# One-block buffers for streamed weight rows, and a second table stage whose activation loads and products are queued behind the first

## The chip, the cores and the metric

The kernel runs on one core of one Trainium2 chip. The metric is device time in microseconds (us) of one execution, as the median of several runs of the same program; lower is better. The engines are named as the profile names them: PE is the matrix engine and PEld its weight load, DVE the vector engine, ACT the scalar engine, POOL the engine that issues the gathers here, SP the engine that issues most of the other transfers. SPq and ACTq are the instruction queues of SP and ACT, which issue DMAs in order.

## The reference, cut to what matters

Two layers. Each layer runs four mixers on 512 tokens (256 context, 256 latent), then a feed-forward network that chooses experts by product keys. Only the feed-forward part and the weight loads are touched.

```python
def block(xb):                                   # 128 tokens at a time
    qry = (xb @ wq).reshape(PEER_BLOCK, PEER_HEADS, 2, PEER_DKEY)
    s = jnp.einsum('thpk,hpnk->thpn', qry, sub_keys)
    sv, si = lax.top_k(s, PEER_TOPK)
    ...
    eidx = jnp.take_along_axis(cand_i, fpos, axis=-1)   # 16384 experts, 8 heads x 16 chosen
    gate = jax.nn.softmax(fs, axis=-1)
    act = jax.nn.gelu(jnp.einsum('td,thkd->thk', xb, u[eidx]), approximate=False)
    w = gate * act
    return jnp.einsum('thk,thkd->td', w, v[eidx])
```

The modulation of each layer, silu(c) @ w_ada + b_ada, is a second product of which the kernel does some columns inside the feed-forward stage of layer 0. The last layer's feed-forward part runs on the 256 latent tokens alone.

## The kernel before

The feed-forward part is computed densely: all 16384 experts, as 128 blocks of 128, for most tokens. It has two table stages. In the **first table's stage** (`u_blocks`) the rows of u are multiplied with the tokens: for each block of 128 experts, 24 matmuls (8 pieces of the model width, each in three products of high and low halves), then a gelu on ACT; two blocks make a pair, and the pair's activations go to a DRAM scratch `ad` by a DMA that ACT issues. In the **second table's stage** (`v_blocks`) a pair's activations come back from `ad` into the tile `va`, the gates come from another DRAM scratch `gd` into `vg`, DVE multiplies them, ACT and DVE split the product into a high and a low half (`wt`), and PE multiplies with the rows of v into eight accumulators `f`.

Rows of both tables come from HBM into the tile `raw`. ACT copies them to a rounded high half and DVE subtracts to get the low half (tiles `spl`, 10 buffers of one block each, shared in the first stage with gathered rows). `raw` has two buffers of 1 MB, each for two blocks in the table stages and for one 256-column weight chunk elsewhere (`wdma`).

The first tokens of each layer (128 in layer 0, 32 in layer 1, `APART`) are not in the dense product. Their chosen rows are gathered one per partition by POOL (`tokens_apart`), 256 gathers in layer 0: DVE makes a dot product with a u row (line 1415) or adds a scaled v row to `facc` (line 1422). `rows_to` decides how many gathers have been written into the program by each pair: 144 of layer 0's (`PHASE1`) by the end of the first table's stage, the rest over the second.

While the first stage runs, DVE and PE also build the gates (`gate_hot`, `gates`), which go to `gd`. In layer 0 the second stage carries 32 rows of the modulation (`ada_row`): a 512 KB load `adaw` and one or two DVE products each, with the constant `csb` (1 MB) loaded and passed through a sigmoid ahead of them.

The order within each engine's queue is made by a planner, which simulates the program and may move an instruction ahead of those written before it. `pin` puts an instruction behind the one written just before it on its engine. Instructions on an engine run in order, so one that waits holds back all behind it. Before the change the loads and products of `v_blocks` and the load of `csb` aren't pinned.

Of the kernel before, what the change touches and what calls it, by code (L numbers as in the profile page):

```python
# [18 lines left out]
L = 2  # L19
# [5 lines left out]
MAGIC = 12582912.0  # L25
GSCALE = 32768.0

RAW, SPL, WQS = 2, 10, (6, 5)
AHEAD = 3
PIECE = 3  # L30
F_ML, F_NA, F_MLA, F_SW = (1.3, 2.0), (1.0, 1.2), (1.2, 1.2), (1.2, 1.0)
# [22 lines left out]
class Kernel:  # L54
# [39 lines left out]
    def build(self):  # L94
        tc, nc, A = self.tc, self.nc, self.A
        with ExitStack() as es:
            self.cst = es.enter_context(tc.tile_pool(name="cst", bufs=1))
            self.dram = es.enter_context(tc.tile_pool(name="scr", bufs=1, space=bass.MemoryType.DRAM))
            self.raw = es.enter_context(tc.tile_pool(name="raw", bufs=RAW, reuse_waits="tile"))
            self.spl = es.enter_context(tc.tile_pool(name="spl", bufs=SPL, reuse_waits="tile"))  # L100
            cst = self.cst
            self.xt = cst.tile([128, KD, TA], F32, name="xt")
            self.cc = cst.tile([128, KD, 2], F32, name="cc")
            nc.sync.dma_start(self.cc, A["cc"])
            self.con = cst.tile([128, C_N], F32, name="con")
            nc.sync.dma_start(self.con[:, 0:128], A["con"][:, 0:128])
            self.ident = self.con[:, C_ID:C_ID + 128]
            self.ng = cst.tile([128, 5, KD], F32, name="ng")
            nc.scalar.dma_start(self.ng, A["ng"])
            self.badat = cst.tile([128, L, 6, KD], F32, name="badat")  # L110
            nc.scalar.dma_start(self.badat, A["bada"])
            self.small = cst.tile([128, 64], F32, name="small")
            nc.scalar.dma_start(self.small, A["small"])
            self.ones = cst.tile([128, 128], F32, name="ones")
            nc.vector.memset(self.ones, 1.0)
            self.mhalf = cst.tile([128, 4], F32, name="mhalf")
            nc.gpsimd.memset(self.mhalf, -0.5)
            self.cmb = cst.tile([4, 2], F32, name="cmb")
            nc.vector.tensor_add(self.cmb, self.ident[0:4, 0:2], self.ident[0:4, 2:4])
            self.mod = {}  # L120
            self.ms = cst.tile([128, 4], F32, name="ms")
            self.wd = [TA - APART[0], TC - APART[1]]
            self.gd = [self.dram.tile([self.wd[l] // 32, 128, 128, 32], F32, name=f"gd{l}") for l in range(L)]
            self.ad = [self.dram.tile([128, 128, self.wd[l]], F32, name=f"ad{l}") for l in range(L)]
            for l in range(L):
                self.mixers(l)
                if self.stop == ("mix", l):
                    return
                self.peer(l)
                if self.stop == ("peer", l):  # L130
                    return
            self.final()
# [162 lines left out]
    def ada_row(self, w, junk, csb, l, n, nv):  # L295

        nc = self.nc
        if l not in self.mod:
            self.mod[l] = self.cst.tile([128, 6, KD, 2], F32, name=f"mod{l}")
            nc.gpsimd.memset(self.mod[l], 0.0)  # L300
        s, k = divmod(n, KD)
        nc.sync.dma_start(w, self.A["wadat"][l, n])
        for j in range(nv):
            o = self.mod[l][:, s, k, j:j + 1]
            self.pin(nc.vector.scalar_tensor_tensor(junk, w, 1.0, csb[:, j], op0=ALU.mult, op1=ALU.mult, accum_out=o))
        nc.vector.tensor_add(self.mod[l][:, s, k, :nv], self.mod[l][:, s, k, :nv], self.badat[:, l, s, k:k + 1].to_broadcast([128, nv]))
# [83 lines left out]


    def raw_tile(self):
        return self.wraw.tile([128, 2048], F32, name="raw")

    def spl_tile(self):
        return self.wspl.tile([128, 1024], F32R, name="spl")

    def wdma(self, src, nk=KD):
        w = self.raw_tile().rearrange("p (k c) -> p k c", c=256)
        self.nc.sync.dma_start(w[:, :nk], src)  # L400
        return w

    def pin(self, ins, on=True):
        return self.tc.keep_in_program_order(ins) if on else ins

    def gload(self, src):

        w = self.raw_tile()[:, 0:1024].rearrange("p (k c) -> p k c", c=128)
        self.nc.sync.dma_start(w, src[:, :, 0:128])
        return w  # L410

# [631 lines left out]
    def peer(self, l):  # L1043
# [7 lines left out]
        with ExitStack() as es:  # L1051
# [19 lines left out]
            with ExitStack() as e1:  # L1071
# [4 lines left out]
                with ExitStack() as e2:  # L1076
                    ep2 = e2.enter_context
                    self.s = ep2(tc.tile_pool(name=f"ps_s{l}", bufs=QS[l], reuse_waits="tile"))
                    self.sm = ep2(tc.tile_pool(name=f"ps_sm{l}", bufs=2, reuse_waits="tile"))
                    local = [ep2(tc.tile_pool(name=f"ps_{n}{l}", bufs=b, reuse_waits="tile")) for n, b in (("wr", 2), ("ws", WQS[l]))]  # L1080
                    kp = ep2(tc.tile_pool(name=f"ps_k{l}", bufs=1, reuse_waits="tile"))
                    self.psum = ep2(tc.tile_pool(name=f"ps_p{l}", bufs=3, space=PSUM, reuse_waits="tile"))
                    psk = ep2(tc.tile_pool(name=f"ps_psk{l}", bufs=3, space=PSUM, reuse_waits="tile"))
# [33 lines left out]
                with ExitStack() as e2:  # L1117
# [24 lines left out]

                    def u_next():
                        u_pair()
                        rows_to(PHASE1[l] * (used[0] - u0) // (64 - u0))
                    for n, _ in enumerate(routes[t0]):
                        if n % RN[l] == 0:
                            u_next()
# [30 lines left out]
                with ExitStack() as e2:  # L1179
# [3 lines left out]
                    acc = [pf.tile([128, 512], F32, name=f"f{d}") for d in range(KD)]  # L1183
                    extra = []
                    if l == 0:
                        self.csb = self.vp.tile([128, 2, 1024], F32, name="csb", bufs=1)
                        nc.sync.dma_start(self.csb, A["ccb"])
                        for j in range(2):
                            sgb = self.junk
                            self.pin(nc.scalar.activation(sgb, self.csb[:, j], AF.Sigmoid))  # L1190
                            nc.vector.tensor_mul(self.csb[:, j], self.csb[:, j], sgb)
                        extra = [(0, n, 2) for n in range(40, 48)] + [(1, n, 2) for n in range(16)] + [(1, n, 1) for n in range(40, 48)]
                    if apart:
                        rows = ep2(tc.tile_pool(name=f"rows{l}", bufs=ROWS, reuse_waits="tile"))
# [1 line left out]
                    for n, i in enumerate(self.v_order(l)):  # L1196
                        rows_to(PHASE1[l] + (2 * apart - PHASE1[l]) * n // 58 if n < 58 else 300)
                        self.v_blocks(l, n, i, acc, ts, w - wd)
                        if extra and n % 2 == 0:
                            self.ada_row(self.vp.tile([128, 1024], F32, name="adaw", bufs=1), self.junk, self.csb, *extra.pop(0))  # L1200
            for k in range(KD):
                self.dump(f"xp{l}_{k}", self.xt[:, k])
# [234 lines left out]
    def u_prep(self, l):  # L1437
# [3 lines left out]
        if n == 128:  # L1441
            return
        self.unext += 1
        if n % 2 == 0:
            self.u = self.raw.tile([128, 2048], F32, name="raw").rearrange("p (b k e) -> p b k e", b=2, k=KD)
            nc.sync.dma_start(self.u, self.A["ut"][l, n:n + 2].rearrange("b p k e -> p b k e"))
        uh, ul = (self.spl.tile([128, 1024], F32R, name="spl").rearrange("p (k e) -> p k e", k=KD) for _ in range(2))
        self.pin(nc.scalar.copy(uh, self.u[:, n % 2]), n < 3)  # L1448
        self.pin(nc.vector.tensor_tensor(ul, self.u[:, n % 2], uh.bitcast(F32), op=ALU.subtract), n < 3)  # L1449
        self.uparts.append((uh, ul))  # L1450

    def u_blocks(self, l, i, hh, hl, w):
# [12 lines left out]
                self.mm3(ps[:, :w], uh[:, k], ul[:, k], hh[k], hl[k], k == 0, k == KD - 1)  # L1465
            nc.scalar.activation(a[:, b, :w], ps[:, :w], AF.Gelu)  # L1466
        if not fold:
            nc.scalar.dma_start(self.ad[l][i:i + 2].rearrange("b p t -> p b t"), a[:, :, :w])

    def v_order(self, l):  # L1470

# [9 lines left out]
    def v_blocks(self, l, n, i, acc, ts, off):  # L1481
# [3 lines left out]
        q = slice(off, off + w)  # L1485
        parts = []
        nc, vp = self.nc, self.vp
        v = self.raw.tile([128, 2048], F32, name="raw").rearrange("p (b d) -> p b d", b=2)
        nc.sync.dma_start(v, self.A["v"][l, i:i + 2].rearrange("b p d -> p b d"))
        fold = i < 2 * FOLD[l]  # L1490
        a = self.kept[:, i:i + 2] if fold else vp.tile([128, 2, w], F32, name="va")
        if i % 4 == 0 and not fold:
            self.vg = vp.tile([128, w // 32, 4, 32], F32, name="vg", bufs=2)
            nc.sync.dma_start(self.vg[:, :w // 32].rearrange("p q b t -> p q (b t)"),
                              self.gd[l][:, :, i:i + 4].rearrange("q p b t -> p q (b t)"))
        if not fold:
            nc.sync.dma_start(a[:, :, :w], self.ad[l][i:i + 2].rearrange("b p t -> p b t"))
        wide = l > 0
        wt = vp.tile([128, 2, 2, w], F32R, name="wt")
        wh, wl = wt[:, :, 0], wt[:, :, 1]  # L1500
        if not fold:
            av = a[:, :, :w].rearrange("p b (q t) -> p b q t", t=32)
            nc.vector.tensor_mul(av, av, self.vg[:, :w // 32, i % 4:i % 4 + 2].rearrange("p q b t -> p b q t"))  # L1503
        nc.scalar.copy(wh, a[:, :, :w])
        nc.vector.tensor_tensor(wl, a[:, :, :w], wh.bitcast(F32), op=ALU.subtract)  # L1505
        for b in range(2):
            vh, vl = (self.spl.tile([128, 1024], F32R, name="spl") for _ in range(2))
            nc.scalar.copy(vh, v[:, b])  # L1508
            nc.vector.tensor_tensor(vl, v[:, b], vh.bitcast(F32), op=ALU.subtract)  # L1509
            parts.append((vh, vl, wh[:, b], wl[:, b], wt[:, b].rearrange("p a t -> p (a t)")))  # L1510

        def mm(d, b):
# [73 lines left out]
class Halves:  # L1586
# [5 lines left out]
    def __getitem__(self, x):  # L1592
        if isinstance(x, slice):
            t = self.tiles[x.start // 4]
            return t[:, x.start % 4:x.start % 4 + x.stop - x.start]
        return self.tiles[x[1] // 4][(x[0], x[1] % 4) + tuple(x[2:])]


# [219 lines left out]
```

## Time and profile before

| | us |
|---|---|
| median of 3 runs | 2793.98 |
| lowest and highest run | 2786.86, 2801.69 |
| profiled execution: its own time | 2801.05 |
| profiled execution: span from first to last instruction | 2799.3 |
| PE busy in it | 2628.3 |
| mean granted PE clock (share of full speed) | 0.973 |

The profiled execution is 1.75 us longer than its span and 7.07 us above the median of the runs. In the order of time the span holds: layer 0 mixers to about 450 us, its query and first table's stage to 1175, its second table's stage to about 1700, layer 1 mixers to about 2000, its first stage to about 2429 and its second to about 2780. An idle PE in a stage is time that another engine or a transfer set; the busy share alone doesn't tell which.

### The profile page before, as it was taken

What the parts mean: (1) busy time and instruction counts of PE and PEld (TensorE: products, weight loads), DVE (VectorE), ACT (ScalarE), POOL (GpSimd) and SP (SyncE); (2) the same over time, 40 slices, a digit from 0 to 9 for tenths busy, and PEclk for the clock granted to TensorE, in tenths of its full rate; (3) what the DMA queues carried; (4) which work ended last, traced back from release to release, by engine and by line L of the source; (5) the groups of instructions that cost most, each with busy time, mean ns of one, the idle gap of its engine ahead of it and who ended that gap; (6) DMA issues with size and microseconds to landing.
All of it is one profiled execution on the core that took longest, in us unless ns stands there. A gap on an engine that the chain in (4) does not pass through costs nothing. (4 is left out here: it accounts for less than half of the span.)

```text
span 2799.3 us, 44568 instructions
## 1 busy us (share of the span) xinstructions
PE 2628.3 (94%) x17143; PEld 2407.9 (86%) x17143; DVE 2168.7 (77%) x4499; ACT 1249.8 (45%) x2059; POOL 490.9 (18%) x419
## 2 busy tenths in 40 slices
PE   8989899999999999799999998988999999998998
PEld 5766768999998898799999997767899999898987
DVE  5665757999998886699999886565788777677776
ACT  4564645334344433343333334554545444444443
POOL 0010000003443234233333320000001111111110
PEclk9999899999999999899999999999999999999999
DMA  7110424647998989989999993211535787998984
GB/s 264 69 61 31 166 89 157 220 159 246 347 359 337 340 321 378 338 322 386 382 367 384 372 364 125 76 39 68 201 137 191 270 283 282 333 319 294 333 306 167
DMA packets 275733, 691.48 MB, mean 247 GB/s; under 512 B 18016, under 2 KB 145376, under 8 KB 266048
## 3 DMA queue, kind: packets, MB, share of 16 engines
q1 hardware_dynamic: 196608, 448.12, 45.6%
q0 software_dynamic: 46080, 167.79, 15.9%
q10 hardware_dynamic: 32832, 72.72, 6.9%
q8 instruction: 134, 2.20, 0.3%
q14 instruction: 79, 0.65, 0.1%
HBM read 616.56 MB, written 71.57 MB: 246 GB/s over the span
## 5 line engine op out<-in xcount | busy, mean ns | idle before, releaser
L72 PE MATMUL pu<-h2h,spl 128*128 128x384 f32 (+1 forms) x2048 | 637.8, 311 | 37.1 <-ACT spl L1448 28.0
L74 PE MATMUL pu<-h2h,spl 128*128 128x384 f32 (+1 forms) x2048 | 629.6, 308 | 2.9 <-DVE spl L1449 2.9
L73 PE MATMUL pu<-h2l,spl 128*128 128x384 f32 (+1 forms) x2048 | 630.2, 308 | 0.0
L72 PEld LDWEIGHTS pu<-h2h,spl 128*128 128x128 f32 x2048 | 394.2, 192 | 44.9 <-ACT spl L1448 32.7
L74 PEld LDWEIGHTS pu<-h2h,spl 128*128 128x128 f32 x2048 | 393.5, 192 | 4.8 <-DVE spl L1449 4.6
L73 PEld LDWEIGHTS pu<-h2l,spl 128*128 128x128 f32 x2048 | 394.2, 192 | 0.3
L1509 DVE TENSOR_TENSOR spl<-raw,spl 128x1024 fp32r<-128x1024 f32 x256 | 305.7, 1220 | 98.2 <-ACT spl L1508 92.5
L1448 ACT CAST spl<-raw 128x1024 fp32r<-128x1024 f32 x256 | 266.3, 1051 | 249.2 <-DMA raw<-in_ut 92.3
L1508 ACT CAST spl<-raw 128x1024 fp32r<-128x1024 f32 x256 | 261.9, 1051 | 256.5 <-DMA raw<-in_v 173.6
L1449 DVE TENSOR_TENSOR spl<-raw,spl 128x1024 fp32r<-128x1024 f32 x256 | 311.7, 1224 | 44.1 <-ACT spl L1448 32.6
L73 PE MATMUL f<-wt,spl 128*128 128x384 f32 x1024 | 343.2, 335 | 0.0
L74 PE MATMUL f<-wt,spl 128*128 128x384 f32 x1024 | 336.3, 334 | 0.0
L72 PE MATMUL f<-wt,spl 128*128 128x384 f32 x1024 | 288.4, 337 | 2.1 <-ACT spl L1508 1.9
L1519 PE MATMUL f<-wt,spl 128*128 128x448 f32 x1024 | 251.1, 372 | 17.1 <-ACT spl L1508 11.7
L1409 POOL DMA_INDIRECT spl<-in_un,ix x97 | 131.6, 1357 | 704.8 <-DVE fp L1263 241.6
L1466 ACT ACTIVATE act<-pu 128x384 f32<-128x384 f32 (+1 forms) x216 | 93.7, 436 | 299.3 <-PE pu L74 268.8
L1519 PEld LDWEIGHTS f<-wt,spl 128*128 128x128 f32 x1024 | 186.0, 190 | 33.3 <-ACT spl L1508 15.0
L427 DVE TENSOR_TENSOR spl<-raw,spl 128x512 fp32r<-128x512 f32 (+1 forms) x226 | 149.8, 702 | 64.0 <-ACT spl L423 55.0
L73 PEld LDWEIGHTS f<-wt,spl 128*128 128x128 f32 x1024 | 193.0, 188 | 0.5 <-issue 0.5
L74 PEld LDWEIGHTS f<-wt,spl 128*128 128x128 f32 x1024 | 191.6, 188 | 0.0
L72 PEld LDWEIGHTS f<-wt,spl 128*128 128x128 f32 x1024 | 187.9, 189 | 3.2 <-ACT spl L1508 2.2
L1409 POOL DMA_INDIRECT row<-in_vn,ix x87 | 125.7, 1445 | 369.6 <-DVE facc L1422 313.0
(326 smaller groups left out, 5029.2 us busy)
## 6 DMA issues: line engine op xcount, KB each, us to landing
raw<-in_ut SPq DMA_DIRECT2D x128, 1024.0 KB
raw<-in_v SPq DMA_DIRECT2D x128, 1024.0 KB
ad<-act ACTq DMA_DIRECT2D x64, 384.0 KB
gd<-gstage ACTq DMA_DIRECT2D x12, 2048.0 KB
vg<-gd SPq DMA_DIRECT2D x32, 768.0 KB
va<-ad SPq DMA_DIRECT2D x64, 384.0 KB
raw<-in_win SPq DMA_DIRECT2D x22, 1024.0 KB
raw<-in_wq SPq DMA_DIRECT2D x16, 1024.0 KB
```

Of the source, the lines that this page charges most:

```text
L72: mm(ps, ah, bh, start=first, stop=False, **kw)
L73: mm(ps, ah, bl, start=False, stop=False, **kw)
L74: mm(ps, al, bh, start=False, stop=last, **kw)
L427: return eng.tensor_tensor(p[1][o], w[:, o], p[0][o].bitcast(F32), op=ALU.subtract)
L1409: nc.gpsimd.indirect_dma_start(r, None, tabs[which], bass.IndirectOffsetOnAxis(ix[:, s:s + 1], 0))
L1448: self.pin(nc.scalar.copy(uh, self.u[:, n % 2]), n < 3)
L1449: self.pin(nc.vector.tensor_tensor(ul, self.u[:, n % 2], uh.bitcast(F32), op=ALU.subtract), n < 3)
L1466: nc.scalar.activation(a[:, b, :w], ps[:, :w], AF.Gelu)
L1508: nc.scalar.copy(vh, v[:, b])
L1509: nc.vector.tensor_tensor(vl, v[:, b], vh.bitcast(F32), op=ALU.subtract)
L1519: nc.tensor.matmul(acc[d][:, off:off + 2 * w], vh[:, c], both, start=first, stop=last)
```

## The change

- `raw` becomes four buffers of 512 KB, one block each, in the same memory. Each block of u and of v has a load of its own; weight chunks are loaded as two halves (`wdma` returns `Halves`).
- The scratch `ad` is laid out so that the two blocks of a pair lie side by side in each partition: a run of 3072 bytes in layer 0 and 1792 in layer 1, where there were two runs of half that.
- In the second table's stage the loads of `vg` and `va`, the product on DVE and the split of the product on ACT and DVE are pinned for the first two pairs; the loads and splits of the rows of v are not.
- The load of `csb` and its sigmoid move from ahead of the second stage to behind its second pair, pinned; the modulation rows start at the third pair, with one at pair 3 besides the even ones (32 as before), and their loads are pinned.
- `rows_to` in the first stage reaches its 144 gathers (26 in layer 1) three pairs before the stage's end.

```diff
-RAW, SPL, WQS = 2, 10, (6, 5)
+RAW, SPL, WQS = 4, 10, (6, 5)
...
-            self.ad = [self.dram.tile([128, 128, self.wd[l]], F32, name=f"ad{l}") for l in range(L)]
+            self.ad = [self.dram.tile([64, 128, 2, self.wd[l]], F32, name=f"ad{l}") for l in range(L)]
...
-        nc.sync.dma_start(w, self.A["wadat"][l, n])
+        self.pin(nc.sync.dma_start(w, self.A["wadat"][l, n]))
...
-        return self.wraw.tile([128, 2048], F32, name="raw")
+        return self.wraw.tile([128, 1024], F32, name="raw")
...
-        w = self.raw_tile().rearrange("p (k c) -> p k c", c=256)
-        self.nc.sync.dma_start(w[:, :nk], src)
-        return w
+        w = [self.raw_tile().rearrange("p (k c) -> p k c", c=256) for _ in range(2)]
+        for t, k in zip(w, (0, 4)):
+            self.nc.sync.dma_start(t[:, :min(nk - k, 4)], src[:, k:min(nk, k + 4)])
+        return Halves(w)
...
-                        rows_to(PHASE1[l] * (used[0] - u0) // (64 - u0))
+                        rows_to(min(PHASE1[l], PHASE1[l] * (used[0] - u0) // (61 - u0)))
...
-                        self.csb = self.vp.tile([128, 2, 1024], F32, name="csb", bufs=1)
-                        nc.sync.dma_start(self.csb, A["ccb"])
-                        for j in range(2):
-                            sgb = self.junk
-                            self.pin(nc.scalar.activation(sgb, self.csb[:, j], AF.Sigmoid))
-                            nc.vector.tensor_mul(self.csb[:, j], self.csb[:, j], sgb)
...
-                        if extra and n % 2 == 0:
+                        if extra and n == 1:
+                            self.csb = self.vp.tile([128, 2, 1024], F32, name="csb", bufs=1)
+                            self.pin(nc.sync.dma_start(self.csb, A["ccb"]))
+                            for j in range(2):
+                                sgb = self.junk
+                                self.pin(nc.scalar.activation(sgb, self.csb[:, j], AF.Sigmoid))
+                                nc.vector.tensor_mul(self.csb[:, j], self.csb[:, j], sgb)
+                        if extra and n > 1 and (n % 2 == 0 or n == 3):
...
-        if n % 2 == 0:
-            self.u = self.raw.tile([128, 2048], F32, name="raw").rearrange("p (b k e) -> p b k e", b=2, k=KD)
-            nc.sync.dma_start(self.u, self.A["ut"][l, n:n + 2].rearrange("b p k e -> p b k e"))
+        u = self.raw.tile([128, 1024], F32, name="raw").rearrange("p (k e) -> p k e", k=KD)
+        nc.sync.dma_start(u, self.A["ut"][l, n])
...
-            nc.scalar.dma_start(self.ad[l][i:i + 2].rearrange("b p t -> p b t"), a[:, :, :w])
+            nc.scalar.dma_start(self.ad[l][i // 2], a[:, :, :w])
...
-        v = self.raw.tile([128, 2048], F32, name="raw").rearrange("p (b d) -> p b d", b=2)
-        nc.sync.dma_start(v, self.A["v"][l, i:i + 2].rearrange("b p d -> p b d"))
+
+        def pin(ins):
+            return self.pin(ins, n < 2)
+        v = [self.raw.tile([128, 1024], F32, name="raw") for _ in range(2)]
+        for b in range(2):
+            nc.sync.dma_start(v[b], self.A["v"][l, i + b])
...
-            nc.sync.dma_start(a[:, :, :w], self.ad[l][i:i + 2].rearrange("b p t -> p b t"))
+            pin(nc.sync.dma_start(a[:, :, :w], self.ad[l][i // 2]))
...
-            nc.vector.tensor_mul(av, av, self.vg[:, :w // 32, i % 4:i % 4 + 2].rearrange("p q b t -> p b q t"))
-        nc.scalar.copy(wh, a[:, :, :w])
-        nc.vector.tensor_tensor(wl, a[:, :, :w], wh.bitcast(F32), op=ALU.subtract)
+            pin(nc.vector.tensor_mul(av, av, self.vg[:, :w // 32, i % 4:i % 4 + 2].rearrange("p q b t -> p b q t")))
+        pin(nc.scalar.copy(wh, a[:, :, :w]))
+        pin(nc.vector.tensor_tensor(wl, a[:, :, :w], wh.bitcast(F32), op=ALU.subtract))
```

The load of `vg` is pinned in the same way.

## Rows read from the trace of the kernel before

**Rows 1.** Windows by stage: busy us of each engine, PE clock, DMA share, GB/s.

```profile
850.00:1080.00 230.00, 215.99 (x1494) 205.85 (x1493) 194.54 (x257) 93.74 (x148) 81.89 (x61) 0.97 0.90 335
1080.00:1175.00 95.00, 73.98 (x397) 71.44 (x395) 50.73 (x57) 25.42 (x36) 34.59 (x30) 0.89 0.98 359
1175.00:1205.00 30.00, 28.13 (x152) 27.81 (x153) 26.36 (x30) 14.93 (x16) 1.68 (x1) 0.94 0.69 233
1205.00:1690.00 485.00, 485.00 (x2800) 485.00 (x2800) 435.52 (x536) 171.97 (x182) 164.08 (x107) 1.00 1.02 370
2150.00:2405.00 255.00, 242.00 (x2311) 240.10 (x2310) 199.35 (x289) 123.83 (x214) 37.19 (x23) 0.98 0.79 276
2405.00:2445.00 40.00, 34.70 (x264) 33.27 (x264) 19.44 (x24) 13.66 (x23) 8.91 (x8) 0.91 1.01 366
2445.00:2745.00 300.00, 284.22 (x1772) 265.56 (x1771) 223.36 (x258) 140.98 (x169) 37.34 (x33) 1.00 0.89 310
```

**Rows 2.** Timeline of PE at layer 0's change of stage; idle time and releaser in brackets.

```profile
1133.12 0.69 PE L72 MATMUL pu<-h2h,spl 128*128 128x384 f32 x1 [15.81 <-ACT spl L1448]
1139.36 0.41 PE L73 MATMUL pu<-h2l,spl 128*128 128x384 f32 x1
```

**Rows 3.** Timeline of SP's queue there.

```profile
1093.80 16.51 SPq L302 DMA_DIRECT2D adaw<-in_wadat  x1
1114.81 9.84 SPq L1446 DMA_DIRECT2D raw<-in_ut  x2
1158.83 24.69 SPq L1489 DMA_DIRECT2D raw<-in_v  x4
```

**Rows 4.** Timeline of DVE there.

```profile
1107.21 1.22 DVE L1449 TENSOR_TENSOR spl<-raw,spl 128x1024 fp32r<-128x1024 f32 x1
1123.19 0.96 DVE L1503 TENSOR_TENSOR va<-va,vg 128x768 f32<-128x768 f32 x1 [14.76 <-DMA va<-ad]
1125.05 0.96 DVE L1505 TENSOR_TENSOR wt<-va,wt 128x768 fp32r<-128x768 f32 x1 [0.90 <-ACT wt L1504]
```

**Rows 5.** Timeline of ACT there.

```profile
1122.66 0.49 ACT L1466 ACTIVATE act<-pu 128x384 f32<-128x384 f32 x1 [13.14 <-DMA vg<-gd]
1124.18 0.83 ACT L1504 CAST wt<-va 128x768 fp32r<-128x768 f32 x1 [1.03 <-DVE va L1503]
1132.03 1.99 ACT L1448 CAST spl<-raw 128x1024 fp32r<-128x1024 f32 x2 [4.29 <-DMA raw<-in_ut]
```

**Rows 6.** Chain of work that ended last, layer 1: start, length, what.

```profile
2419.31 17.36 DMA va<-ad
2506.58 7.78 DMA raw<-in_v
```

**Rows 7.** Layer 1's first stage, 2150 to 2405: a wait, and groups of PE.

```profile
ACT spl L1448 <- DMA raw<-in_ut: 58.3, 26, 6.6
...
L72 PE MATMUL pu<-h2h,spl 128*128 128x224 f32 x624 | 175.7, 282 | 5.3 <-ACT act L1466 5.3
L1368 PE MATMUL pg<-at,bt 128*128 128x128 f16 x434 | 31.7, 221 | 7.7 <-DVE kept L1375 7.7
```

**Rows 8.** Layer 1's second stage, 2445 to 2745: a wait, and groups of PE.

```profile
ACT spl L1508 <- DMA raw<-in_v: 118.7, 51, 5.1
...
L1519 PE MATMUL f<-wt,spl 128*128 128x448 f32 x886 | 203.6, 369 | 11.8 <-ACT spl L1508 11.7
L1521 PE MATMUL f<-wt,spl 128*128 128x224 f32 x886 | 121.1, 274 | 4.0 <-DVE spl L1509 3.9
```

**Rows 9.** Layer 0's gathered rows on DVE, 689.5 to 1117; gelus before 689.5.

```profile
L1415 DVE SCALAR_TENSOR_TENSOR junk<-spl,ht 128x1024 f32<-128x1024 f32 x63 | 77.1, 1224 | 12.4 <-DMA spl<-in_un,ix 12.4
L1422 DVE SCALAR_TENSOR_TENSOR facc<-spl,wt,facc 128x1024 f32<-128x1024 f32 x52 | 66.6, 1281 | 6.4 <-DMA spl<-in_vn,ix 6.3
...
L1466 ACT ACTIVATE act<-pu x37: 477/492/494, 469.6 to 687.7; 128x384 f32<-128x384 f32 x37
```

**Rows 10.** Loads of v on SP: issue ns min/median/max, first and last.

```profile
L1489 SPq DMA_DIRECT2D raw<-in_v x128: 367/368/1634, 1158.8 to 2763.4; - x128
```

More of the change, by code (lines that the diff above doesn't have):

```diff
@@ L406, in gload @@
     def gload(self, src):
-        w = self.raw_tile()[:, 0:1024].rearrange("p (k c) -> p k c", c=128)
+        w = self.raw_tile().rearrange("p (k c) -> p k c", c=128)
         self.nc.sync.dma_start(w, src[:, :, 0:128])
@@ L1079, in peer @@
                     self.sm = ep2(tc.tile_pool(name=f"ps_sm{l}", bufs=2, reuse_waits="tile"))
-                    local = [ep2(tc.tile_pool(name=f"ps_{n}{l}", bufs=b, reuse_waits="tile")) for n, b in (("wr", 2), ("ws", WQS[l]))]
+                    local = [ep2(tc.tile_pool(name=f"ps_{n}{l}", bufs=b, reuse_waits="tile")) for n, b in (("wr", 4), ("ws", WQS[l]))]
                     kp = ep2(tc.tile_pool(name=f"ps_k{l}", bufs=1, reuse_waits="tile"))
@@ L1443, in u_prep @@
         self.unext += 1
-        if n % 2 == 0:
-            self.u = self.raw.tile([128, 2048], F32, name="raw").rearrange("p (b k e) -> p b k e", b=2, k=KD)
-            nc.sync.dma_start(self.u, self.A["ut"][l, n:n + 2].rearrange("b p k e -> p b k e"))
+        u = self.raw.tile([128, 1024], F32, name="raw").rearrange("p (k e) -> p k e", k=KD)
+        nc.sync.dma_start(u, self.A["ut"][l, n])
         uh, ul = (self.spl.tile([128, 1024], F32R, name="spl").rearrange("p (k e) -> p k e", k=KD) for _ in range(2))
-        self.pin(nc.scalar.copy(uh, self.u[:, n % 2]), n < 3)
-        self.pin(nc.vector.tensor_tensor(ul, self.u[:, n % 2], uh.bitcast(F32), op=ALU.subtract), n < 3)
+        self.pin(nc.scalar.copy(uh, u), n < 3)
+        self.pin(nc.vector.tensor_tensor(ul, u, uh.bitcast(F32), op=ALU.subtract), n < 3)
         self.uparts.append((uh, ul))
@@ L1493, in v_blocks @@
             self.vg = vp.tile([128, w // 32, 4, 32], F32, name="vg", bufs=2)
-            nc.sync.dma_start(self.vg[:, :w // 32].rearrange("p q b t -> p q (b t)"),
-                              self.gd[l][:, :, i:i + 4].rearrange("q p b t -> p q (b t)"))
+            pin(nc.sync.dma_start(self.vg[:, :w // 32].rearrange("p q b t -> p q (b t)"),
+                                  self.gd[l][:, :, i:i + 4].rearrange("q p b t -> p q (b t)")))
         if not fold:
-            nc.sync.dma_start(a[:, :, :w], self.ad[l][i:i + 2].rearrange("b p t -> p b t"))
+            pin(nc.sync.dma_start(a[:, :, :w], self.ad[l][i // 2]))
         wide = l > 0
@@ L1502, in v_blocks @@
             av = a[:, :, :w].rearrange("p b (q t) -> p b q t", t=32)
-            nc.vector.tensor_mul(av, av, self.vg[:, :w // 32, i % 4:i % 4 + 2].rearrange("p q b t -> p b q t"))
-        nc.scalar.copy(wh, a[:, :, :w])
-        nc.vector.tensor_tensor(wl, a[:, :, :w], wh.bitcast(F32), op=ALU.subtract)
+            pin(nc.vector.tensor_mul(av, av, self.vg[:, :w // 32, i % 4:i % 4 + 2].rearrange("p q b t -> p b q t")))
+        pin(nc.scalar.copy(wh, a[:, :, :w]))
+        pin(nc.vector.tensor_tensor(wl, a[:, :, :w], wh.bitcast(F32), op=ALU.subtract))
         for b in range(2):
             vh, vl = (self.spl.tile([128, 1024], F32R, name="spl") for _ in range(2))
-            nc.scalar.copy(vh, v[:, b])
-            nc.vector.tensor_tensor(vl, v[:, b], vh.bitcast(F32), op=ALU.subtract)
+            nc.scalar.copy(vh, v[b])
+            nc.vector.tensor_tensor(vl, v[b], vh.bitcast(F32), op=ALU.subtract)
             parts.append((vh, vl, wh[:, b], wl[:, b], wt[:, b].rearrange("p a t -> p (a t)")))
@@ L1595, in __getitem__ @@
             return t[:, x.start % 4:x.start % 4 + x.stop - x.start]
+        if isinstance(x[1], slice):
+            return self.tiles[x[1].start // 4][:, x[1].start % 4:x[1].start % 4 + x[1].stop - x[1].start]
         return self.tiles[x[1] // 4][(x[0], x[1] % 4) + tuple(x[2:])]
```

## The prediction

> **What bounds the kernel now.** I read the stages first. In layer 0's second table stage PE is busy for all 485 us and the DMA engines are at a share of 1.02 [rows 1]: PE sets the time, and transfers have almost nothing to spare. Elsewhere PE has gaps: 14.0 us of 230 in layer 0's first stage beside the gates, 21.0 of the 95 that end in the change of stage, 1.9 in the 30 after it, 13.0 of 255 in layer 1's first stage, 5.3 around its change of stage and 15.8 of 300 in its second stage [rows 1]. A buffer change can gain only there. The mixers I leave alone: their loads are the same bytes in the same memory.
>
> Then I read who waits in the worst gap. PE stands for 15.81 us on a split by ACT [rows 2]. ACT makes that split when rows of u land at about 1132.0 [rows 5]. Those rows could have been asked for when DVE had read the old ones, at 1107.21 + 1.22 = 1108.4 [rows 4]; SP issued them at 1114.8, since its queue had been stuck for 16.51 us on the load of `adaw`, a thing of the second stage [rows 3]. They took until 1132, 17 us. Meanwhile DVE sat 14.76 us on a product of the second stage and ACT 13.14 us on a gates' transfer [rows 4, 5]: the planner had placed the second stage's work ahead of the first's last splits, and its inputs were late. After the gap PE ran slowly: the 19 matmuls recorded from 1133.12 to 1139.36 (one record seems missing) step by 0.32 us for 384 columns, the 1.2 GHz level, half speed [rows 2]. That is 3.1 us lost of 6.24.
>
> Last I read layer 1. Its chain of waits is a loop: rows land, ACT copies, DVE subtracts, the buffer is free, the next 1 MB takes 7.78 us [rows 6]. ACT waited for rows of v 51 times, 118.7 us in all, 2.3 each; for rows of u 26 times, 58.3, 2.2 each [rows 7, 8]. PE sees only part: 11.8 + 4.0 us in the second stage, and in the first 5.3 behind an eviction on ACT (which runs in order behind the waiting copies) and 7.7 behind the gate products [rows 7, 8].
>
> **The change, part by part.** The sum is against the profiled execution, 2801 us, 7 above the median of the runs; I take the same 7 off at the end.
>
> *Pins at layer 0's change of stage.* Loads of `va`, `vg`, `csb` and `adaw` no longer stand in front of u's last rows on SP, and no product waits in DVE and ACT in front of their splits. The 15.8 and 3.1 us go: -18.9. Bounds: 0, if something else is late for the same PE, and -21.0 - 3.1 = -24.1 if all of that stretch's idle time goes too.
>
> *What the pins add.* A pinned instruction follows the one written before it. For `wt`'s copy on ACT that is the first stage's last gelu and its DMA issue, so PE can't begin the second stage until gelu (0.49), copy (0.83) and DVE's low half (0.96) are through [rows 4, 5]: 2.3 us, with the issue of a DMA (0.37, [rows 10]) at most 2.7. PE had none of this. On SP the pinned loads queue behind the first two loads of v, which wait for buffers of u's last blocks; behind them wait later loads of v. Those buffers came free from 1158.8 on [rows 3], and the stage ends at 1175 [rows 1]: a lead of 16 us. The longest such landing in the chain is 17.36 [rows 6], so the first product is late by about 1. I take +3.5; bounds +2 (half hidden) and +10 (landing after a lead that is 7 us shorter).
>
> *csb and its sigmoid behind the second pair.* ACT could block on 1 MB that lands late. Splits are up to five blocks ahead (10 `spl` buffers, two a block), and the DMA share right after the change was 0.69 [rows 1]: 0.31 of 30 us is 9 us of transfers, at 370 GB/s 3.4 MB. I take 0; without that cover a landing of 7.78 us for 1 MB [rows 6] would be bare, so 0 to +8. The 32 modulation rows stay 32.
>
> *Four buffers, layer 1.* The first block's buffer is freed one subtraction earlier (1.22 us, [rows 4]) and half the bytes must land before ACT can copy. If latency and transfer share the 7.78 us evenly, the copy comes 1.2 + 1.9 = 3.1 us earlier, more than the mean waits of 2.2 and 2.3. So most of the raw-bound idle time goes: in the second stage I take half of 15.8, -8, since DVE's other work and `va` are in the same loop; in the first stage -5 of 13.0, mostly the 5.3. Bounds 0 and -28.8. At layer 1's change of stage (5.3 idle) nothing: its first product uses activations kept on chip, and the load of `va` was behind v's first load already. ±3.
>
> *Four buffers, layer 0.* Splits there wait on other things than landing rows, and in the second stage PE never waits: 0. SP issues 256 more loads of 0.37 us [rows 10], 94 us spread over some 2000 with its queue mostly waiting for buffers: 0.
>
> *Gathers three pairs earlier.* 37 gelus stood before 689.5, about 18 pairs and a half [rows 9], so 144 gathers spread over 42 pairs and no longer 45: 3.43 a pair for 3.20. At 1.22 to 1.28 us each [rows 9] that is 0.23 x 1.25 x 42 = 12 us of DVE work, and 5 MB, moved forward into stretches where DVE was busy 194.5 of 230 and DMA at 0.90 [rows 1], and away from the change of stage. I take +2; bounds 0 and +12.
>
> *Scratch layout.* Half as many runs for `ad` and `va`, same bytes. It relieves the DMA engines by an amount that no row isolates, where they are not the bound. 0; bounds -5 (1% of the 485 us) and 0.
>
> Sum: -18.9 + 3.5 - 8 - 5 + 2 = -26.4. 2801 - 26 = 2775 for a profiled execution, 2768 for the median: 0.95% faster. About 0.5%, 14 us, is what can be told from no change here.
>
> **The rivals.** *The burst only moves.* The loads held back (`csb` 1.0 MB, `adaw` 0.5, three `vg` of 0.75, four `va` of 0.375) are 5.25 MB, 14 us at 366 to 370 GB/s. If they all come between the last rows of u and the second product of v, the gap reopens there: the change of stage gains 18.9 - 3.5 - 14 = 1, the sum is -12 and the time 2782. For it: a DMA share of 0.98 and 1.02 on both sides. Against: the 0.69 between [rows 1], and gathers that have ended three pairs before. Chance 0.15.
>
> *Layer 1 doesn't move.* The wait of ACT passes to DVE's queue or to `va`, which is in the chain with 17.36 us [rows 6]: -26 + 13 = -13, 2781, at the edge of no change. Chance 0.15, a third of it just faster.
>
> *Smaller loads deliver less.* In layer 0's second stage DMA is at 1.02 with PE never idle [rows 1]. If 512 KB loads lose p per cent of delivery there, PE becomes DMA-bound and the stage grows by 4.85 us for each. It decides against the change from 26/4.85 = 5.4%; at 9% the time is 2768 + 44 = 2812, slower by 0.6%. Against it: each partition's run of a block is 4 KB before and after, gathers of 512 KB shared that stage at 370 GB/s, and four loads may be under way for two. Chance 0.18, which holds the other slower ways too. The Trainium skill speaks for this rival: "DMA: Bandwidth & Descriptors", section "Bandwidth", asks for at least 1 MiB a DMA, and its section on the anatomy of one DMA fits 2.0 us fixed a transfer. An estimate from that page: one load alone takes 3.2 us for 512 KB and 4.4 for 1 MB, so a pair would lose 2.0 us if its two loads never overlapped, 128 us over 64 pairs; the 370 GB/s at 1.02 [rows 1], on loads of which many were 512 KB or less, speaks against taking it whole.
>
> **How the numbers follow.** Forecast 0.52; burst 0.15; layer 1 unmoved 0.15; slower 0.18. Faster: 0.52 + 0.05 = 0.57. Same: 0.15 + 0.10 = 0.25. Slower: 0.18. Low end: all idle time named gone, -24.1 + 2 - 28.8 = -51, with the 3 that layer 1's change of stage could lose -48, so 2746. High end: the smaller loads at 7%, 2768 + 34 = 2802. That leaves out the worst of the slower cases, about 1.3 in 10, and little below. The forecast's own range is 2750 to 2779.
>
> **What would show it.** In the trace after: no gap over 5 us on PE in the 95 us that end layer 0's first stage; no load of `adaw` or `csb` on SP ahead of u's last; one gap of 2 to 4 us where `f` begins, put down to ACT or DVE `wt`; in layer 1 ACT's waits for `raw` well under 118.7 and 58.3, and PE idle near 8 of 300. I'm wrong if PE shows idle time in layer 0's second stage, or if the same 15 us stand at its first pairs put down to `va` or `vg`, or if the gathers make the first stage's idle time grow past 20.

## The result, and the profile after

The median went from 2791.32 us (four runs) to 2761.05 (four runs, 2757.97 to 2772.51): a ratio of 0.9901, 95% interval 0.9873 to 0.9929. That is 30 us. The two profiled executions lie further apart, spans of 2799.3 and 2757.7 us, since before's was at the upper end of its runs and after's at the lower of its own. Differences between single profiles below are therefore read for place and kind; sizes are taken from ratios. One of the six runs of e1_raw_only below took 4247 us at a granted clock of 0.559, against 2769 to 2779 us for the others, and is left out of its ratio.

Windows by stage of the kernel after: layer 0's first and second table stage, then layer 1's. The columns are as in [rows 1]: the window and its length, then busy us and count of PE, PEld, DVE, ACT and POOL, then PE's granted clock, the DMA share and GB/s. The stages are cut at the first gelu, the first and the last matmul into `f`.

```profile
474.20:1150.10 675.90, 650.21 (x4145) 621.89 (x4145) 609.43 (x1463) 270.22 (x414) 204.06 (x149) 1.00 0.85 314
1150.10:1690.00 539.90, 538.96 (x3090) 537.68 (x3091) 470.46 (x577) 189.92 (x203) 167.17 (x107) 0.99 0.97 350
...
1983.30:2415.70 432.40, 411.44 (x3776) 408.72 (x3774) 344.59 (x796) 211.00 (x358) 47.80 (x31) 0.98 0.73 250
2415.70:2741.60 325.90, 325.26 (x2065) 310.05 (x2066) 253.02 (x294) 156.88 (x191) 36.63 (x33) 0.99 0.88 310
```

The same four stages of the kernel before:

```profile
469.60:1174.20 704.60, 665.36 (x4167) 636.28 (x4166) 604.40 (x1466) 272.09 (x414) 204.59 (x148) 0.98 0.83 303
1174.20:1714.00 539.80, 537.70 (x3089) 536.10 (x3089) 473.67 (x586) 194.15 (x207) 165.77 (x109) 1.00 0.97 350
...
2004.90:2429.00 424.10, 407.60 (x3777) 405.10 (x3775) 338.45 (x786) 209.36 (x354) 45.02 (x30) 0.99 0.70 247
2429.00:2783.30 354.30, 334.04 (x2066) 312.12 (x2067) 258.05 (x304) 160.10 (x196) 38.42 (x34) 0.99 0.85 296
```

Layer 0's first stage lost 28.7 us and layer 1's second 28.4; layer 0's second did not move; layer 1's first grew by 8.3. What came before the first gelu grew by 4.6, and layer 1's mixers by 2.6. The sum is -41.6. Less than half of the 28.7 in layer 0's first stage is idle time of PE (39.2 to 25.7 us, length less busy time); its busy time fell too, by 15.2, at a granted clock of 1.00 for 0.98. In layer 1's second stage PE's idle time fell from 20.3 to 0.6.

At layer 0's change of stage SP's queue now holds v's first rows, then pinned loads, then `csb`, and `adaw` last; there is no 16.51 us stand as in [rows 3] (timeline of SP's queue):

```profile
1127.32 3.19 SPq L1494 DMA_DIRECT2D raw<-in_v  x2
...
1131.13 3.20 SPq L1502 DMA_DIRECT2D va<-ad  x1
...
1139.85 0.47 SPq L1196 DMA_DIRECT2D csb<-in_ccb  x1
...
1151.47 0.38 SPq L302 DMA_DIRECT2D adaw<-in_wadat  x1
```

PE's gap of 15.81 us [rows 2] is gone. One gap remains, where `f` begins (timeline of PE, idle time in brackets):

```profile
1150.09 2.93 PE L72 MATMUL f<-wt,spl 128*128 128x384 f32 x8 [6.15 <-ACT wt L1509]
```

In layer 1 ACT's waits for landing rows of v fell from 118.7 us [rows 8] to 14.1 in an equal stretch (waits, 2437 to 2737). For rows of u they fell from 58.3 [rows 7] to 20.8 (2130 to 2415, 285 us for 255), but the gate products kept PE longer there, 11.5 us for 7.7:

```profile
ACT spl L1513 <- DMA raw<-in_v: 14.1, 18, 2.1
...
ACT spl L1449 <- DMA raw<-in_ut: 20.8, 14, 3.9
...
L1370 PE MATMUL pg<-at,bt 128*128 128x128 f16 x446 | 33.2, 222 | 11.5 <-DVE kept L1377 11.3
```

### The profile page after: what moved, and what is told of

It is laid out like the page before. It is cut to its first block, busy times and chain, and to the rows that moved or that the text cites. A ratio compares the mean times of both kernels' runs of the same rounds, so it can differ in the third digit from the quotient of the medians.

```text
span 2757.7 us, 45475 instructions
## 1 busy us (share of the span) xinstructions
PE 2617.6 (95%) x17143; PEld 2402.7 (87%) x17143; DVE 2174.1 (79%) x4499; ACT 1242.5 (45%) x2057; POOL 492.8 (18%) x419
## 5 line engine op out<-in xcount | busy, mean ns | idle before, releaser
L73 PE MATMUL f<-wt,spl 128*128 128x384 f32 x1024 | 343.1, 335 | 0.0
L74 PE MATMUL f<-wt,spl 128*128 128x384 f32 x1024 | 343.0, 335 | 0.0
L1524 PE MATMUL f<-wt,spl 128*128 128x448 f32 x1024 | 310.1, 375 | 3.2 <-DVE wt L1510 3.2
L72 PE MATMUL f<-wt,spl 128*128 128x384 f32 x1024 | 302.8, 337 | 7.1 <-ACT wt L1509 7.1
L1526 PE MATMUL f<-wt,spl 128*128 128x224 f32 x1016 | 247.8, 266 | 0.0
L1524 PEld LDWEIGHTS f<-wt,spl 128*128 128x128 f32 x1024 | 190.7, 189 | 17.1 <-DVE wt L1510 3.4
L72 PEld LDWEIGHTS f<-wt,spl 128*128 128x128 f32 x1024 | 189.5, 189 | 8.2 <-ACT wt L1509 7.7
L73 PEld LDWEIGHTS f<-wt,spl 128*128 128x128 f32 x1024 | 193.1, 189 | 0.5 <-issue 0.5
```

The costliest lines, as they stand in the source:

```text
L72: mm(ps, ah, bh, start=first, stop=False, **kw)
L73: mm(ps, ah, bl, start=False, stop=False, **kw)
L74: mm(ps, al, bh, start=False, stop=last, **kw)
L1524: nc.tensor.matmul(acc[d][:, off:off + 2 * w], vh[:, c], both, start=first, stop=last)
L1526: nc.tensor.matmul(acc[d][:, q], vl[:, c], wh, start=False, stop=False)
```

## The experiments

Twelve kernels, in three groups that each shared a chip and the runs of the kernel before. Ratios are to those runs. The planner orders each kernel anew, so an edit can also move instructions that it doesn't name; no run holds the order fixed. "Gap" is the longest idle time of PE at layer 0's change of stage, and where it stands; the last columns are the lengths of the stages in the profiled execution, in us.

| kernel | ratio, 95% interval | gap | L0 first | L0 second | L1 first | L1 second |
|---|---|---|---|---|---|---|
| before | 1 | 15.8 in u | 704.6 | 540.0 | 424.1 | 354.3 |
| the change | 0.9901, 0.9873 to 0.9929 | 6.2 at `f` | 675.9 | 539.9 | 432.4 | 325.9 |
| e1_raw_only | 0.9935, 0.9918 to 0.9952 | 16.7 in u | 683.3 | 552.4 | 410.3 | 337.1 |
| e2_pins_only | 1.0014, 1.0001 to 1.0027 | 25.7 at `f` | 703.1 | 537.8 | 427.2 | 347.1 |
| e3_no_raw | 1.0025, 1.0007 to 1.0042 | 2.1 in u | 695.7 | 535.9 | 433.3 | 343.1 |
| e4_no_pins | 0.9963, 0.9947 to 0.9979 | 17.0 in u | 692.7 | 542.9 | 432.4 | 327.2 |
| e5_no_pace | 0.9897, 0.9881 to 0.9912 | 22.2 at `f` | 686.8 | 539.0 | 420.2 | 329.3 |
| e6_no_layout | 0.9897, 0.9876 to 0.9919 | 6.2 at `f` | 676.8 | 539.2 | 440.7 | 326.8 |
| e7_csb_front | 0.9967, 0.9954 to 0.9980 | 9.7 at `f`, 5.4 in u | 688.6 | 543.4 | 432.3 | 325.7 |
| e8_split_loads | 0.9904, 0.9889 to 0.9920 | 13.7 in u | 683.9 | 539.6 | 412.8 | 338.9 |
| e9_split_parts | 1.1808, 1.1780 to 1.1836 | 15.1 in u | 743.0 | 793.3 | 477.2 | 473.3 |
| e10_pace0 | 0.9840, 0.9818 to 0.9863 | 6.2 at `f` | 676.7 | 539.9 | 427.1 | 327.6 |
| e11_big_split_pace0 | 0.9903, 0.9880 to 0.9926 | 2.6 at `f` | 690.2 | 537.2 | 425.3 | 332.4 |
| e12_load_pins | 0.9892, 0.9872 to 0.9913 | 6.2 at `f` | 678.0 | 538.5 | 426.7 | 328.5 |

**Buffers alone, pins alone, and each left out.** My theory was that the pins own layer 0's change of stage and the buffers layer 1's second stage, each for itself. e1_raw_only is the kernel before with this part of the change:

```diff
-RAW, SPL, WQS = 2, 10, (6, 5)
+RAW, SPL, WQS = 4, 10, (6, 5)
...
+        u = self.raw.tile([128, 1024], F32, name="raw").rearrange("p (k e) -> p k e", k=KD)
+        nc.sync.dma_start(u, self.A["ut"][l, n])
...
+        v = [self.raw.tile([128, 1024], F32, name="raw") for _ in range(2)]
+        for b in range(2):
+            nc.sync.dma_start(v[b], self.A["v"][l, i + b])
```

> The four one-block buffers alone; pins, csb, scratch layout and gather pace as before. Theory A (buffers own layer 1's second stage, pins own layer 0's change of stage): that second stage shrinks from 352 us to about 325, the PE gap of 10 us or more at layer 0's change of stage stays; ratio to before 0.990 to 0.995. Rival B (one-block loads also get u's last rows out in time, pins are idle): gap gone too, ratio 0.988 to 0.990. Rival C (layer 1's second stage is shorter because its start is in order, by the pins): stage stays at 345 or more, ratio 0.998 to 1.002.

e2_pins_only is the kernel before with the pins and the new place of `csb` and of the modulation rows:

```diff
+            return self.pin(ins, n < 2)
...
+                        if extra and n == 1:
...
+        self.pin(nc.sync.dma_start(w, self.A["wadat"][l, n]))
```

> The pins, and csb and the modulation rows behind the second pair; 1 MB buffers of two blocks, layout and pace as before. Theory A: gap at layer 0's change of stage goes from 15.8 to under 7 us, layer 1's second stage stays at 345 to 352; ratio 0.992 to 0.996. Rival B: gap stays, ratio 0.998 to 1.002. Rival C: gap gone and layer 1's second stage near 325, ratio 0.985 to 0.990.

e3_no_raw and e4_no_pins are the kernel after, with the edits of e1 and of e2 taken back.

> The whole change but for the buffers: 1 MB of two blocks again. Theory A: layer 1's second stage back at 345 to 352 us, layer 0's change of stage without a gap over 7; ratio to before 0.992 to 0.997. Rival B: 0.998 to 1.002. Rival C: 0.985 to 0.990.

> The whole change but for the pins and the place of csb and of the modulation rows. Theory A: a gap of 10 us or more at layer 0's change of stage, layer 1's second stage near 325; ratio to before 0.990 to 0.996. Rival B: as the whole change, 0.988 to 0.992. Rival C: 0.996 to 1.002.

The buffers alone give 0.65%, with the gap still there, as Theory A had it; layer 1's second stage went to 337, where it had 325. The pins alone give nothing, and the profile shows why. Timelines of PE, of SP's queue and of ACT in e2_pins_only:

```profile
1172.35 2.93 PE L72 MATMUL f<-wt,spl 128*128 128x384 f32 x8 [25.66 <-ACT wt L1509]
...
1134.03 10.85 SPq L1502 DMA_DIRECT2D va<-ad  x1
...
1162.25 1.04 ACT L1513 CAST spl<-raw 128x1024 fp32r<-128x1024 f32 x1 [14.10 <-DMA raw<-in_v]
```

PE no longer stands inside the first stage; it stands 25.66 us where the second begins. The loads held back come out in one burst (10.85 us for SP to get one `va` load out), the first 1 MB of v rows land at about 1143.9 and the next, asked for at 1147.6 behind them, at 1162. ACT waits 14.10 us for these, and the product's copy stands behind on ACT. So the stall was moved, not removed. Taking the pins out of the whole change brings the gap of 17.0 back and costs 0.6%, taking the buffers out costs 1.2%. The parts don't add. Theory A holds for the places: with the pins out the gap stands in u whichever buffers there are, and layer 1's second stage is 343 us or more with 1 MB loads and 339 or less with smaller ones. It fails for the pins' worth: e2's ratio is Rival B's ("gap stays"), e3's lies outside every range, and e4's at the edge between A and C. e3 is the plainest: no gap over 2.1 us is left at layer 0's change of stage, and nothing is gained. In its profile PE still idles 29.5 of that first stage's 695.7 us, and layer 1's first stage is 9 us longer than before.

**Which of the small edits count.** Each is the kernel after with one edit taken back. e5_no_pace:

```diff
-                        rows_to(min(PHASE1[l], PHASE1[l] * (used[0] - u0) // (61 - u0)))
+                        rows_to(PHASE1[l] * (used[0] - u0) // (64 - u0))
```

> The whole change with the gathers at their old pace (144 and 26 spread to the first stages' very ends). Theory A (the faster pace costs DVE and transfers in both first stages, more than the two changes of stage get back): first stages shorter by 5 to 15 us in layer 0 beside its gap and by 10 to 20 in layer 1; ratio to before 0.985 to 0.990. Rival B (the pace is needed, since the second stage's first loads must not meet gathers): a gap of 15 us or more where layer 0's second stage begins, ratio 0.993 to 0.998. Rival C (the pace is nothing): 0.989 to 0.992.

e6_no_layout:

```diff
-            nc.scalar.dma_start(self.ad[l][i // 2], a[:, :, :w])
+            nc.scalar.dma_start(self.ad[l][i:i + 2].rearrange("b p t -> p b t"), a[:, :, :w])
```

> The whole change with the scratch as before, two runs of half the length per partition. Theory A (layout is nothing, no engine waits for the transfers saved): 0.989 to 0.992. Rival B (fewer, longer runs relieve saturated transfers by 1 to 2 per cent): 0.994 to 0.999, with ACT and PE waiting more for landing rows in layer 0. Rival C (layout is what makes layer 1's first stage longer): under 0.988, that stage near 410 us.

e7_csb_front puts `csb` and the first modulation row back ahead of the second stage, without pins on them:

```diff
-                        if extra and n == 1:
...
+                        self.csb = self.vp.tile([128, 2, 1024], F32, name="csb", bufs=1)
+                        nc.sync.dma_start(self.csb, A["ccb"])
```

> The whole change, but csb and the modulation rows as before: csb ahead of the second stage, first row at its first pair, no pins on them; pins of the first two pairs stay. Theory A (the gap needs both: SP's queue behind csb and adaw, and products in DVE and ACT): a gap between 5 and 15 us comes back at layer 0's change of stage; 0.992 to 0.996. Rival B (the products alone made the gap): as the whole change, 0.989 to 0.992. Rival C (adaw on SP alone made it): gap of 15 or more, 0.996 to 0.999.

The layout is worth nothing measurable. The pace is worth nothing as a sum, but of two parts: at the old pace the gap at `f` is 22.2 us (Rival B's sign), while layer 1's first stage takes 420 and no longer 432 (Theory A's). What the pace clears shows on ACT, in the timeline of e5_no_pace: its copies of v's rows take buffers of `spl`, as the gathered rows do, and one of them waits until a gathered row has landed.

```profile
1155.48 1.04 ACT L1513 CAST spl<-raw 128x1024 fp32r<-128x1024 f32 x1 [7.19 <-DMA spl<-in_un,ix]
```

`csb` and the modulation rows carry all that the pins give, as far as ratios tell: with them in front 0.66% is lost, as much as without any pins (0.62%, e4), and the gap is split in two, 5.4 us in u and 9.7 at `f`. The gap is as Theory A has it, the ratio is Rival C's. Which of the two loads counts, and what the products in DVE and ACT cost by themselves, no run separates.

**Size of a load, or release of a buffer?** e8_split_loads is the kernel before, with two buffers of 1 MB as ever, each filled by two loads (the weight chunks too):

```diff
-            nc.sync.dma_start(self.u, self.A["ut"][l, n:n + 2].rearrange("b p k e -> p b k e"))
+            for b in range(2):
+                nc.sync.dma_start(self.u[:, b], self.A["ut"][l, n + b])
...
-        nc.sync.dma_start(v, self.A["v"][l, i:i + 2].rearrange("b p d -> p b d"))
+        for b in range(2):
+            nc.sync.dma_start(v[:, b], self.A["v"][l, i + b])
```

> The kernel before, with its two 1 MB buffers but each filled by two loads of 512 KB: the size of a load without the finer release. Theory A (layer 1's second stage gains by a buffer being free one block earlier): that stage stays at 345 to 354 us; ratio 0.998 to 1.003. Rival B (half loads landing one after another are enough): stage at 325 to 337, ratio 0.992 to 0.996. Rival C (smaller loads deliver less): layer 0's second stage over 550 us, ratio over 1.004.

This was the surprise. Halving the loads alone, with no buffer free any earlier, gives 0.96%, as much as the whole change. It is Rival B in kind; the ratio is lower than its range. My theory of the earlier release falls as the main cause. The halved weight chunks aren't the gain: up to the first gelu e8 took 477.5 us for 469.6 before, and layer 1's mixers 290.3 for 290.7. Window of e8's second stage in layer 1, then a wait there (2420 to 2720):

```profile
2404.10:2743.00 338.90, 329.62 (x2066) 311.30 (x2067) 257.83 (x303) 164.61 (x196) 48.59 (x34) 0.99 0.88 309
```

```profile
ACT spl L1515 <- DMA raw<-in_v: 109.7, 88, 5.0
```

The DMA engines did not deliver more for their busy time: 309 GB/s at a share of 0.88 is 351 per unit of share, against 296 at 0.85, 348, before. But ACT's waits for rows are 1.25 us each (109.7 in 88), where they were 2.3 (118.7 in 51): shorter, and one for each block. A copy now starts on the first block before the second has landed. In that stage both landings of a pair are on record for 42 pairs: the second comes 1.33 us after the first (median), and in 39 of them ACT has begun to copy the first block by then. One such pair, in the timeline of ACT in e8_split_loads:

```profile
2537.43 1.05 ACT L1515 CAST spl<-raw 128x1024 fp32r<-128x1024 f32 x1 [1.95 <-DMA raw<-in_v]
2538.75 1.05 ACT L1515 CAST spl<-raw 128x1024 fp32r<-128x1024 f32 x1 [0.27 <-DMA raw<-in_v]
```

Without pins the finer release adds nothing to this: e1, with four buffers, stands at 0.9935. In e1 PE idles 12.1 us in layer 0's second stage, for 2.1 before: the sign that I had named for being wrong, though the whole change doesn't show it (0.9).

e9_split_parts was to test what the earlier start of the copy is worth: two half loads again, but each of 64 partitions of both blocks, so that any copy needs both (v's rows and the weight chunks are cut in the same way).

```diff
+            for h in (slice(0, 64), slice(64, 128)):
+                nc.sync.dma_start(self.u[h], self.A["ut"][l, n:n + 2, h].rearrange("b p k e -> p b k e"))
```

> The kernel before, each 1 MB load cut into two loads of 64 partitions (both blocks in each): size and count of e8_split_loads, the same 4 KB runs, but the copy of the first block has to wait for both. Theory A (the gain of half loads is that ACT can start on the first block when half the bytes are there): no gain, ratio 0.997 to 1.004, layer 1's second stage 347 to 356 us. Rival B (smaller loads, two at a time, land sooner as such): as e8, 0.988 to 0.993, stage 330 to 342.

It was 18% slower and answers another question. Layer 0's second stage in its windows:

```profile
1240.00:2030.00 790.00, 623.40 (x3075) 596.91 (x3074) 475.13 (x585) 189.46 (x205) 161.69 (x108) 0.86 0.93 240
```

The DMA engines were as busy as ever, 0.93, and moved 240 GB/s, where the kernel before moved 350 at 0.97 over the same stage. So the cut itself, by partitions, made each byte dearer, and whether the copies waited for both halves can't be read from it. That e8's copies start earlier is seen in its trace; that its gain comes from this is argued, since no run takes the early start away alone.

**The faster pace in layer 0 alone, with either kind of buffer.** e10_pace0 is the kernel after with

```diff
-                        rows_to(min(PHASE1[l], PHASE1[l] * (used[0] - u0) // (61 - u0)))
+                        rows_to(min(PHASE1[l], PHASE1[l] * (used[0] - u0) // ((61, 64)[l] - u0)))
```

> The whole change with the faster gather pace in layer 0 only. Theory A (in layer 0 the pace clears the start of the second stage, in layer 1 it only puts DVE behind rows that land late): layer 0 as with the whole change (second stage begins near 1150), layer 1's first stage 410 to 422 us for 432; ratio 0.983 to 0.988. Rival B (layer 1 needs it as well: what its first stage gains the second loses): 0.988 to 0.992.

and e11_big_split_pace0 is e10 with e8's two large buffers in place of the four.

> As e10_pace0, but with two buffers of 1 MB, each filled by two half loads: pins, layout and pace of e10, without the finer release of buffers. Theory A (half loads are the gain, one-block buffers add little): within 0.004 of e10's ratio, layer 1's second stage within 8 us of e10's. Rival B (one-block buffers matter where the second stage starts, since its loads find room earlier): a gap of over 12 us at layer 0's second stage and a ratio 0.005 or more above e10's.

e10 is the best version: 0.9840, whose interval ends below where the whole change's begins. Its profiled execution is no shorter than the change's (2758.2), and its layer 1 shows a first stage of 427 for 432, inside what two executions may differ by; the gain is in the medians, and its place isn't shown. Nor did the whole change run in e10's group; e12 below, which is the change but for two pins, did, and stands at 0.9892. e11 is 0.63% above it with a gap of only 2.6: the two large buffers cost it in layer 0's first stage, 690 for 677. So the finer release is worth something once the pins are there, though in another stage than I had said; neither of e11's alternatives had that.

Layer 1 has a gap of its own where `f` begins, since the pins hold for its first two pairs too. In the whole change it is 3.17 us, put down to DVE's `wt`. In e5 and e10, where layer 1 keeps the old pace, it is 11.0 and 9.9 (timeline of PE in e10_pace0):

```profile
2415.05 0.74 PE L1524 MATMUL f<-wt,spl 128*128 128x448 f32 x1 [9.89 <-DVE wt L1510]
```

So the earlier gathers shorten the gap in layer 1 as well, but by these profiles the stage before it pays more than that. Without the gap at its end, layer 1's first stage is 427 to 436 us in the six kernels with the faster pace there, and 409 to 424 in the seven others (e9 left out).

**What is left of the gap.** e12_load_pins takes the pins off the two splits of the product:

```diff
-        pin(nc.scalar.copy(wh, a[:, :, :w]))
+        nc.scalar.copy(wh, a[:, :, :w])
```

> The whole change with the loads and DVE's product pinned, but not the two splits of the product (ACT's copy, DVE's low half). Theory A (the gap left where f begins in layer 0, 6.15 us, is mostly the pinned copy behind the last gelu): gap 2 to 4 us there, ratio 0.987 to 0.991. Rival B (the gap is the landing of va and vg): gap stays at 5 to 7, 0.989 to 0.992. Rival C (a copy moved ahead of the last gelu blocks ACT): gap over 8, 0.992 or more.

The gap stays at 6.15 us, so the pinned copy doesn't set it; in layer 1 the gap of 3.17 is gone in e12. Nor does the landing of `va` set it: the first load, issued at 1131.13, took 9.5 us and was there at 1140.6. Timelines of ACT and of DVE in the kernel after:

```profile
1143.98 0.49 ACT L1467 ACTIVATE act<-pu 128x384 f32<-128x384 f32 x1 [2.10 <-PE pu L74]
1144.87 1.99 ACT L1513 CAST spl<-raw 128x1024 fp32r<-128x1024 f32 x2 [0.40 <-ACT act L1467]
...
1145.94 2.36 DVE L1514 TENSOR_TENSOR spl<-raw,spl 128x1024 fp32r<-128x1024 f32 x2 [2.27 <-ACT spl L1513]
1148.22 0.95 DVE L1508 TENSOR_TENSOR va<-va,vg 128x768 f32<-128x768 f32 x1
```

ACT copies v's first rows, which had landed by 1137.0, only after the last gelu; DVE's two subtractions wait for those copies; the product stands behind them with no wait of its own, then ACT's copy of it. It is a matter of order, and of ACT's more than of DVE's. In e3 and e11 the two subtractions precede the product on DVE as well, but ACT makes its two copies before the last gelu (at 1163.50 and 1161.88, with the gelu at 1167.28 and 1165.28), and the gap at `f` is 1.9 and 2.6. This compares traces; no run changes that order alone.

## Why the prediction was right, and where it wasn't

The total was forecast at -26 us, a ratio of 0.9905; 0.9901 was measured. That they agree so closely is partly luck, as the steps show:

- *Pins at layer 0's change of stage, -18.9.* The gap and the slow matmuls after it went as described, and no load of `adaw` stands ahead of u's last. Taken out of the whole change the pins cost 0.62%, some 17 us, near my -18.9 + 3.5. That this is a gain of its own is wrong: e2 has all of it and no gain, and my rival "the burst only moves" was right for the pins alone. It is the pace that brings the gap at `f` down: with the smaller loads but the old pace it is 22.2 (e5), with 1 MB loads and the pace 1.9 (e3). Closing it is worth nothing with 1 MB loads (e3), and 0.57% with smaller ones (e10 for e5, in two groups). The slow matmuls were sized too small: I took 3.1 us behind one gap, and PE's busy time in that stage fell by 15.2 at a higher granted clock.
- *What the pins add, +3.5.* 6.15 measured in layer 0. I put it down to the pinned copy and a late landing; e12 and the timelines point to the order on ACT and DVE. In layer 1, where I had put the change of stage at nothing within 3, the pins add 3.17, and some 10 at the old pace.
- *csb behind the second pair, 0.* Its sigmoid blocked nothing; layer 0's second stage is 539.9 for 540.0. I had counted its absence from the front in the first term without pricing it; e7 shows 0.66%, some 18 us.
- *Four buffers, layer 1, -13.* Layer 1's two stages together lost 20: -28.4 in the second, where I had halved 15.8, and +8.3 in the first, where I had -5. The wait I named did shrink, to 14.1 us, but the mechanism had two parts, and smaller loads alone, which need no extra buffer, took 27 us off the two stages (e8). In the second stage all of PE's idle time went, where I had taken half. The loss in the first stage goes with the faster pace, which I had priced for layer 0 only.
- *Four buffers, layer 0, 0.* Wrong: e1 and e8 end layer 0's first stage 11 and 13 us sooner after the start than before does (first matmul into `f` at 1163.3 and 1161.4 for 1174.2) with the gap still in it. The stage itself is 21 us shorter in both; e1 gives 12 of them back in the second stage, e8 none. I had read that the splits there wait on other things than landing rows. Before, ACT waited there six times for rows of u, 17.8 us in all; in e8 it is 1.0 and in e1 1.8.
- *The mixers, left alone.* I put their loads at nothing. Where the weight chunks are halved over all partitions the first gelu comes at 474 to 482 us; with 1 MB loads it comes at 469 to 473 (before, e2, e3). So the halves may cost up to 12 us there; the profiles also differ in granted clock, and no run separates the two.
- *Gathers, +2, and layout, 0.* Both net to nothing (e5, e6), the gathers by two effects that cancel.
- *Smaller loads deliver less.* They don't, as long as they span all partitions: 351 GB/s per unit of share against 348. In layer 0's second stage, where I feared for them, 350 GB/s at 0.97 stand before and after, so of the estimate of 128 us nothing showed.

So the sum held because two gains that were too small (buffers in layer 0, layer 1's second stage) met costs that were missing (pace and pins in layer 1, perhaps the mixers). That is luck. The direction rests on firmer ground: the smaller loads alone give the gain (e8), and without them it is gone (e3).

## What to carry to other kernels

Before buying a buffer, try two loads into the one that is there: a consumer that works block by block can start on the first block before the second has landed (1.3 us here), and smaller loads alone were worth as much as the whole change. Holding work back to clear a queue moves its transfers into one burst; look at what the next stage needs first, and judge the hold together with what thins that burst. When parts of a change are worth keeping by stage, try them by stage: the earlier gathers shortened the gap at both layers' changes of stage, but in layer 1 they cost the stage before it more, and the fastest kernel has them in layer 0 alone.

## What the runs showed of the hardware

Loads that span half the partitions are dear even two at a time: 512 KB over 64 partitions brought layer 0's second stage down to 240 GB/s at a DMA share of 0.93 (e9), where 512 KB over 128 partitions left it at 350 at 0.97 (e8, and the kernel after). The Trainium skill says so: "SBUF — State Buffer", section "Can I just issue two DMAs to hit both halves?", holds that a transfer reaches all of SBUF's DMA ports only if it alone spans all 128 partitions. The trace agrees in the rate, 240 GB/s for 350; it has no row on ports. The Trainium skill's rule of at least 1 MiB a DMA, in "DMA: Bandwidth & Descriptors", section "Bandwidth", did not decide here: loads of 512 KB gave a ratio of 0.9904 (e8).
